# Norm statistics placed later at the heads of sublayers, and sparse-attention keys and values from 256 columns with DMA copies

## The chip, the core and the metric

The kernel runs on one core of one Trainium2 chip. The metric is the device time of one execution in microseconds, from three runs of the kernel before; the profile is of one further execution.

## The reference, cut to what matters

Two transformer blocks run one after the other on one sequence of 256 tokens and width 1024, all in float32. The first block has two layers, each with a mixer of four branches (sparse attention, retention, a linear recurrence, a short convolution), a cross-attention and an MLP. The second has an even layer (recurrence and attention, then a SwiGLU) and an odd one (gated linear attention, then eight experts). Every sublayer starts with a norm and a projection; the sparse attention takes six column groups of 64 from its projection:

```python
def rms_norm(x, g):
    xf = x.astype(jnp.float32)
    y = xf * lax.rsqrt(jnp.mean(xf * xf, axis=-1, keepdims=True) + RMS_EPS)
    return (y * g.astype(jnp.float32)).astype(x.dtype)
...
h = rms_norm(x, ln_mix_pre[l])
z = h @ w_in[l]
z_q, z_kv, z_g, z_ret, z_rwkv, z_conv, z_gate = split_cols(z, IN_SIZES)
...
k_c, v_c, k_s, v_s, k_w, v_w = jnp.split(kv, 6, axis=-1)
k_cmp = jnp.einsum('bnld,lde->bne', k_c[:, cmp_idx] + cmp_pe, cmp_w[0])
v_cmp = jnp.einsum('bnld,lde->bne', v_c[:, cmp_idx] + cmp_pe, cmp_w[1])
```

## The kernel before

**Products.** Activations lie feature-major in SBUF: a tile holds 128 features on the partitions and 256 tokens. Each float32 operand is split into a high and a low part, and a product is three matmuls: high by high, high by low, low by high. The weights stream from HBM in loads of 1 MB (`wraw`, issued by SP); each half load is one *unit*, for which ScalarE writes `whi` and VectorE `wlo` (lines 372 and 373, the *weight split*). There are four buffers of each, and `Weights.get` prepares up to three units ahead. A unit of `fm_units` gives 128 output features in 8 x 3 = 24 matmuls of 256 columns; two units fill one PSUM bank, which an eviction on VectorE then multiplies by the inverse norm. Units of `tm_units` give token-major results (`vt`, `tv`, `tg`, the cross-attention's `xv`) in two banks. PSUM has three banks for such products (tag mm) and five for the rest (tag b).

**The norm.** The gain is folded into the activations (`scaled` writes `xgh` and `xgl`), and the inverse root mean square is applied at the eviction. `squares` makes the sums of squares on ScalarE and GpSimd (`sq_acc`), `inv_rms` sums them over the partitions on TensorE (two matmuls of one column each), adds epsilon on VectorE (`st_m`) and takes the power on GpSimd (`st_tm_x`); `stat` then broadcasts the result with two matmuls and copies it to SBUF (`st_rep_x`, line 477). `later` puts all of this off to the first eviction that asks for it.

**Heads.** `ramp` takes the first three units of a sublayer and runs them side by side, chunk by chunk, since the chunks of `xgh` and `xgl` are still being made; then come their evictions, with the statistics in front. Nine sublayers begin in this way: two mixers, two cross-attentions, two MLPs, the even mixer, the SwiGLU and the odd mixer. In layer 0's mixer the ramp has one unit.

**The sparse attention.** Its projection is the units q, kcv, ksw, vt, tq, tk and so on. kcv holds the columns of k_c and v_c each twice, and ksw those of k_s and k_w each twice, so that both partition halves hold a copy: the heads lie two to a tile, on partitions 0 to 63 and 64 to 127. The additions `kp` and `vp` (line 1000) read both halves of kcv for the compression, and the scores read both halves of ksw. In layer 0, `bias_tables` also makes the position bias: a product with `c_oh`, a DMA to HBM (`bscr`), a gather back into `merged`, both issued by GpSimd (lines 775 and 777), and two products with `c_flip`.

**Order.** Engines run their instructions in order. Up to the odd layer's output product the scheduler of the tile framework may move an instruction ahead of others of its engine; `weave` sets where the steps of a branch stand between units.

Of the kernel before, what the change touches and what calls it, by code (L numbers as in the profile page):

```python
# [12 lines left out]
F32 = mybir.dt.float32  # L13
# [25 lines left out]
def _cc(w, c0, n=256):  # L39
    nb = n // P  # L40
    return w[:, c0 : c0 + n].reshape(8, P, nb, P).transpose(1, 2, 0, 3).reshape(P, 8 * n)
# [18 lines left out]
def _layout():  # L60
# [3 lines left out]
    def add(key, subs, f):  # L64
        out.append((key, subs, f))

    for l in range(2):
# [7 lines left out]
                add((nm, l, j), two, lambda a, b=base + 256 * j, wi=wi: _cc(wi(a), b))  # L75
        add(("rl", l), (1024,), lambda a, wi=wi: _cc(wi(a), 2444, 128))
        add(("q", l), two, lambda a, wi=wi: _cc(wi(a), 0))
        add(("kcv", l), two, lambda a, wi=wi: _cc(_cols(wi(a), ((256, 64), (256, 64), (320, 64), (320, 64))), 0))
        add(("ksw", l), two, lambda a, wi=wi: _cc(_cols(wi(a), ((384, 64), (384, 64), (512, 64), (512, 64))), 0))
        add(("vt", l), (560, 560), lambda a, wi=wi: _tm(_cols(wi(a), ((448, 64), (576, 64), (640, 12))), 0, 140))  # L80
        add(("tq", l), two, lambda a, wi=wi: _cc(wi(a), 652))
        add(("tk", l), two, lambda a, wi=wi: _cc(wi(a), 908))
# [304 lines left out]
class Net:  # L387
# [78 lines left out]

    def stat(self, parts, tag, copy=True):

        nc = self.nc
        tm = self.inv_rms(parts, tag)  # L470
        ps2 = self.bank()
        for h in range(2):
            self.mm(ps2[:, h * P : h * P + P], tm[:, h : h + 1].to_broadcast([P, P]), self.ident, True, True)
        if not copy:
            return ps2[:, :S], tm
        rep = (self.early if tag == "m" else self.mid).tile([P, S], F32, name="st_rep_" + tag, tag="st_rep_" + tag)
        nc.vector.tensor_copy(rep, ps2[:, :S])
        return rep, tm
# [38 lines left out]

    def later(self, sq, tag):

        made = []  # L520

        def get(i):
            if not made:
                made.extend(self.stat([sq], tag))
            return made[i]

        return (lambda: get(0)), (lambda: get(1))

    def prenorm(self):
# [68 lines left out]
    @staticmethod  # L598
    def ramp(units, n=3):

        held, out, count = [], [], 0
        for u in units:
            if u[0] != "w" or count == n:
                out.append(u)
                continue
            count += 1

            def g(hi, lo, parts=u[3].parts, last=count == n):
                held.append((parts, hi, lo))
                if not last:  # L610
                    return
                for (begin, _, _, i), _, _ in held:
                    begin(i)
                for k in range(8):
                    for (_, step, _, i), h, l in held:
                        step(i, k, h, l)
                for (_, _, end, i), _, _ in held:
                    end(i)

            out.append((*u[:3], g))  # L620
        return out

    def tm_units(self, key, xh, xl, n, evict):
# [166 lines left out]
    def mix_phase(self, l):  # L790
# [58 lines left out]
        def ev_q(ps):  # L849
# [2 lines left out]
            p3 = ps.rearrange("p (c t) -> p c t", c=2)  # L852
            nc.vector.scalar_tensor_tensor(t, p3, 0.125, rep2(), op0=ALU.mult, op1=ALU.mult)

        def ev_vt(h, ps):
            if h == 0:
                st["nv"] = st["a"].tile([P, 2, P], F32, name="nv")
# [19 lines left out]
        if l == 0:  # L877
            src.append(("x", self.load_tables))
            src.append(("x", lambda: st.__setitem__("flip", self.bias_tables(st["a"], st["merged"]))))
        src += self.fm_units(("kcv", l), xh, xl, to_fm("kcv"))  # L880
        src += self.fm_units(("ksw", l), xh, xl, to_fm("ksw"))
        src += self.tm_units(("vt", l), xh, xl, 140, ev_vt)
        units += self.ramp(src, 1 if l == 0 else 3)
        rest = []
        rest += self.fm_units(("tq", l), xh, xl, to_fm("tq"))
        rest += self.fm_units(("tk", l), xh, xl, to_fm("tk"))
        rest += self.tm_units(("tv", l), xh, xl, S, ev_tm("tv"))
        rest += self.tm_units(("tg", l), xh, xl, S, ev_tm("tg"))
# [616 lines left out]
    def xa_phase(self, l):  # L1505
# [82 lines left out]
            return f  # L1588

        qs = [self.fm_units(("xq", l, j), lambda: st["xh"], lambda: st["xl"], ev_q(j)) for j in range(4)]  # L1590
        units += self.ramp(qs[0] + qs[1])
        for j in range(4):
            if j > 1:
                units += qs[j]
# [44 lines left out]
    def mlp_phase(self, l):  # L1639
# [21 lines left out]
        done = lambda n, ps: self.post_evict(n, ps, "ln_mlp_post", l)  # L1661
        second = lambda j: self.second_product(st, ("m2", l, j), j == 0, j == 15, done, (0, 2, 4, 6, 1, 3, 5, 7))
        m1 = [self.fm_units(("m1", l, j), lambda: st["xh"], lambda: st["xl"], ev) for j in range(16)]
        units += self.ramp(m1[0] + m1[1])
        for j in range(2, 16):
            units += m1[j] + second(j - 2)
        units += second(14) + second(15)

        def close():
# [50 lines left out]
    def even_phase(self):  # L1720
# [198 lines left out]
            return [u[0] for u in us], [u[1] for u in us], fox_av(g)  # L1919

        v = [self.tm_units(("ev", j), xh, xl, S, ev_v(j)) for j in range(2)]
        units += self.ramp(fm("xr", 0) + fm("xr", 1))
        first = fm("q", 0) + fm("k", 0) + self.fm_units(("ef",), xh, xl, ev_f, nblk=1) + v[0]
        units += self.weave(first, [load, decay, conv, gates(0), gates(1)])
        a, b, c = heads(0)
        units += self.weave(fm("yr", 0) + fm("yr", 1), [lru, a[0], a[1], b[0], b[1]])
# [12 lines left out]
    def swiglu_phase(self):  # L1939
# [37 lines left out]
        for j in range(11):  # L1977
            u = self.fm_units(("f1", j), lambda: st["xh"], lambda: st["xl"], ev1)
            u += self.fm_units(("f3", j), lambda: st["xh"], lambda: st["xl"], ev3)
            units += self.ramp(u) if j == 0 else u  # L1980
            if j > 0:
                units += second(j - 1)
        units += second(10)
# [9 lines left out]
    def odd_phase(self, moe):  # L1993
# [191 lines left out]
        for j in range(4):  # L2185
            v += self.tm_units(("ov", j), xh, xl, S, ev_v(j))
            g.append(self.tm_units(("og", j), xh, xl, S, ev_g(j)))
        first = self.ramp(first)
        units += first[:5] + self.weave(first[5:], [logits, logs])
        units += self.weave(v, [decays, lambda: self.moe_load(moe), att(0), att(1)])  # L2190
        units += [("x", f) for f in (state, out(0), out(1))]
        units += g[0] + g[1] + [("x", tr(0))] + g[2] + [("x", tr(1))] + g[3] + [("x", tr(2)), ("x", tr(3))]
# [474 lines left out]
```

## Time and profile before

| | us |
|---|---|
| three runs: median (lowest, highest) | 2739.9 (2737.66, 2743.22) |
| profiled execution | 2740.58 |
| span in the profile, first to last instruction | 2738.7 |
| TensorE busy | 2656.7 |
| VectorE busy | 2073.5 |
| ScalarE busy | 1604.9 |
| GpSimd busy | 207.3 |
| mean granted TensorE clock | 0.986 |

The span is the profiled execution without what lies before its first and behind its last instruction, 1.9 us. Busy times are unions of the engine's instructions; matmuls overlap each other, so TensorE's share says that it rarely waits, not that it is at its peak. The names PE, DVE, ACT, POOL and SP in rows stand for TensorE, VectorE, ScalarE, GpSimd and the engine that issues the weight loads.

### The profile page before, as it was taken

To read this page: it belongs to the slowest core of one execution; us is meant where nothing else is said; L and a number is where in the kernel's file an instruction comes from. 1 tells how busy PE (TensorE), PEld (TensorE's weight loads), DVE (VectorE), ACT (ScalarE), POOL (GpSimd) and SP (SyncE) were. 2 spreads that over 40 slices of the span, in tenths; PEclk is the share of its full clock that TensorE was granted. 3 is DMA by queue.
4 is the path that set the end of the run, shared out by engine and by line. 5 is a ranking of instruction groups with operands and counts; after the bars stand their busy time and mean duration, and the time that the engine had idled before them with its cause. 6 is when DMAs were issued, how large, how long until landed. Compare 5 with 4: busy or idle time off the path is not lost.

```text
span 2738.7 us, 44381 instructions
## 1 busy us (share of the span) xinstructions
PE 2656.7 (97%) x17966; PEld 2420.1 (88%) x17966; DVE 2073.5 (76%) x2527; ACT 1604.9 (59%) x2140; POOL 207.3 (8%) x180
## 2 busy tenths in 40 slices
PE   8999998998999999998999999999999999999998
PEld 7989988998989998998999999887887888788876
DVE  5876765556785865556966676899999989999997
ACT  4443645444433544444654456777777777777776
POOL 1032111001022111001010010000000000000000
PEclk9999999999999999999999999999999999999999
DMA  7423434543332543454465444899999989998991
GB/s 253 146 80 132 174 140 165 184 182 136 132 110 89 180 149 123 174 184 150 142 259 211 174 168 161 339 360 350 340 351 357 359 332 358 352 361 334 366 350 68
DMA packets 99887, 614.29 MB, mean 224 GB/s; under 512 B 10521, under 2 KB 20249, under 8 KB 31705
## 3 DMA queue, kind: packets, MB, share of 16 engines
q1 hardware_dynamic: 99496, 610.83, 60.9%
q8 instruction: 143, 2.34, 0.3%
q14 instruction: 72, 0.58, 0.1%
q0 software_dynamic: 176, 0.53, 0.0%
HBM read 610.27 MB, written 1.06 MB: 223 GB/s over the span
## 4 chain that ended last, share of the span: by engine, by line
PE 48%; DVE 3%; ACT 1%; issue 1%; POOL 0%; ACTq 0%; DVEq 0%; POOLq 0%
PE ps_mm L423 31%; PE ps_b L423 16%; PE ps_b L427 1%; DVE wlo L373 1%; ACT whi L372 0%; DVE room L431 0%; DVE mt L2233 0%; DVE acc L2396 0%; POOL st_tm_x L452 0%; DVE room L2079 0%; DVE fv L2585 0%; DVE e L1841 0%; PE ps_r L2480 0%; ACT acc L2491 0%; DVE x L1714 0%
## 5 line engine op out<-in xcount | busy, mean ns | idle before, releaser
L373 DVE TENSOR_TENSOR wlo<-wraw,whi 128x1024 fp32r<-128x1024 f32 (+1 forms) x1133 | 1381.3, 1238 | 390.0 <-ACT whi L372 379.7
L372 ACT ACTIVATE whi<-wraw 128x1024 fp32r<-128x1024 f32 (+1 forms) x1133 | 1181.7, 1055 | 785.7 <-PE ps_mm L423 593.8
L423 PE MATMUL ps_mm<-xgh,whi 128*128 128x256 f32 x2080 | 601.9, 290 | 15.5 <-ACT whi L372 8.6
L423 PE MATMUL ps_mm<-xgh,wlo 128*128 128x256 f32 x2080 | 596.2, 287 | 4.1 <-DVE wlo L373 4.1
L423 PE MATMUL ps_mm<-xgl,whi 128*128 128x256 f32 x2080 | 597.4, 287 | 1.8 <-DVE xgl L507 1.8
L423 PE MATMUL ps_mm<-whi,gx 128*128 128x512 f32 x1792 | 591.1, 399 | 0.0
L423 PEld LDWEIGHTS ps_mm<-xgh,whi 128*128 128x128 f32 x2080 | 402.2, 194 | 21.5 <-ACT whi L372 8.6
L423 PEld LDWEIGHTS ps_mm<-whi,gx 128*128 128x128 f32 x1792 | 337.4, 188 | 79.4 <-issue 0.5
L423 PEld LDWEIGHTS ps_mm<-xgh,wlo 128*128 128x128 f32 x2080 | 400.1, 192 | 5.8 <-DVE wlo L373 5.5
L423 PEld LDWEIGHTS ps_mm<-xgl,whi 128*128 128x128 f32 x2080 | 400.7, 193 | 4.3 <-DVE xgl L507 3.0
L423 PE MATMUL ps_mm<-wlo,gx 128*128 128x512 f32 x896 | 354.9, 396 | 0.2 <-DVE wlo L373 0.2
L423 PE MATMUL ps_b<-whi,room 128*128 128x512 f32 x896 | 294.6, 397 | 0.0
L423 PEld LDWEIGHTS ps_mm<-wlo,gx 128*128 128x128 f32 x896 | 168.7, 188 | 39.1 <-issue 0.7
L423 PEld LDWEIGHTS ps_b<-whi,room 128*128 128x128 f32 x896 | 168.2, 188 | 39.4 <-issue 0.2
L423 PE MATMUL ps_b<-hl,whi 128*128 128x256 f32 x688 | 194.7, 283 | 0.0
L423 PE MATMUL ps_b<-hh,wlo 128*128 128x256 f32 x688 | 194.6, 283 | 0.0
L423 PE MATMUL ps_b<-hh,whi 128*128 128x256 f32 x688 | 194.6, 283 | 0.0
L423 PE MATMUL ps_b<-wlo,room 128*128 128x512 f32 x448 | 176.8, 395 | 0.0
L423 PEld LDWEIGHTS ps_b<-hh,wlo 128*128 128x128 f32 x688 | 132.0, 192 | 0.0
L423 PEld LDWEIGHTS ps_b<-hh,whi 128*128 128x128 f32 x688 | 132.0, 192 | 0.0
L423 PEld LDWEIGHTS ps_b<-hl,whi 128*128 128x128 f32 x688 | 131.9, 192 | 0.0
L423 PEld LDWEIGHTS ps_b<-wlo,room 128*128 128x128 f32 x448 | 84.2, 188 | 19.5 <-issue 0.2
(542 smaller groups left out, 3617.8 us busy)
## 6 DMA issues: line engine op xcount, KB each, us to landing
wraw<-in_w SPq DMA_DIRECT2D x559, 1024.0 KB, 5.5
wrawt<-in_w SPq DMA_DIRECT2D x32, 256.0 KB, 5.2
wraw<-in_w SPq DMA_DIRECT2D x8, 512.0 KB, 5.0
cmpw<-in_cmpw SPq DMA_DIRECT2D x2, 1024.0 KB, 4.8
mem<-in_memt SPq DMA_DIRECT2D x2, 1024.0 KB, 7.7
wraw<-in_w SPq DMA_DIRECT2D x2, 560.0 KB, 4.7
x<-in_xt SPq DMA_DIRECT2D x4, 256.0 KB, 5.0
c_rd<-in_cst SPq DMA_DIRECT2D x2, 512.0 KB, 8.2
```

The costliest lines, as they stand in the source:

```text
L372: nc.scalar.activation(hi[:, c], src[:, c], AF.Copy)
L373: nc.vector.tensor_sub(lo[:, c], src[:, c], hi[:, c].bitcast(F32))
L423: self.nc.tensor.matmul(out, lhsT, rhs, start=start, stop=stop, **kw)
L427: self.nc.tensor.transpose(out, in_, self.ident[:k, :k])
```

## The change

The sums of squares and their broadcast become two steps: `later` gives the net a function `sums`, and `spread` makes the broadcast. `opening` takes the place of `ramp` in all heads but the output products: the first three units still run side by side, the evictions of the first four units are held back, the sums stand behind the unit with number a and the held evictions, with the broadcast in front, behind the unit with number b. In MLPs, mixers and the even head a third product's units stand in between.

kcv and ksw become one product, kn, from 256 columns (k_c, v_c, k_s, k_w once each). Its eviction writes each group on the partition half where it lies, and GpSimd issues a DMA for each group that copies it to the other half. tq moves ahead of vt.

```diff
-        add(("kcv", l), two, lambda a, wi=wi: _cc(_cols(wi(a), ((256, 64), (256, 64), (320, 64), (320, 64))), 0))
-        add(("ksw", l), two, lambda a, wi=wi: _cc(_cols(wi(a), ((384, 64), (384, 64), (512, 64), (512, 64))), 0))
+        add(("kn", l), two, lambda a, wi=wi: _cc(_cols(wi(a), ((256, 64), (320, 64), (384, 64), (512, 64))), 0))
...
     def stat(self, parts, tag, copy=True):
 
+        return self.spread(self.inv_rms(parts, tag), tag, copy)
+
+    def spread(self, tm, tag, copy=True):
+
         nc = self.nc
-        tm = self.inv_rms(parts, tag)
         ps2 = self.bank()
...
-        made = []
+        tm, made = [], []
+
+        def sums():
+            if not tm:
+                tm.append(self.inv_rms([sq], tag))
 
         def get(i):
             if not made:
-                made.extend(self.stat([sq], tag))
+                sums()
+                made.extend(self.spread(tm[0], tag))
             return made[i]
 
+        self.sums = sums
...
+    def opening(self, units, n=3, a=3, held=4, b=4):
+
+
+        out, count, side, ends = [], 0, [], []
+        for u in units:
+            out.append(u)
+            if u[0] != "w":
+                continue
+            if count < held:
+                begin, step, end, i = u[3].parts
+                ends.append((end, i))
+
+                def g(hi, lo, p=u[3].parts, at=count):
+                    side.append((p, hi, lo))
+                    if at < n - 1:
+                        return
+                    for (begin, _, _, i), _, _ in side:
+                        begin(i)
+                    for k in range(8):
+                        for (_, step, _, i), h, l in side:
+                            step(i, k, h, l)
+                    side.clear()
+
+                out[-1] = (*u[:3], g)
+            if count == a:
+                out.append(("x", lambda: self.sums()))
+            if count == b:
+                out += [("x", lambda e=e: e[0](e[1])) for e in ends]
+            count += 1
         return out
...
+        def ev_kn(ps):
+
+            r = st["rep"]()
+            for i, name in enumerate(("kcv", "ksw")):
+                t = st[name] = st["a"].tile([P, 2, S], F32, name=name)
+                for j in range(2):
+                    rows, other = slice(64 * j, 64 * j + 64), slice(64 - 64 * j, 128 - 64 * j)
+                    nc.vector.tensor_mul(t[rows, j, :], ps[rows, i * S : i * S + S], r[rows, :])
+                    nc.gpsimd.dma_start(t[other, j, :], t[rows, j, :])
...
-        src += self.fm_units(("kcv", l), xh, xl, to_fm("kcv"))
-        src += self.fm_units(("ksw", l), xh, xl, to_fm("ksw"))
-        src += self.tm_units(("vt", l), xh, xl, 140, ev_vt)
-        units += self.ramp(src, 1 if l == 0 else 3)
-        rest = []
-        rest += self.fm_units(("tq", l), xh, xl, to_fm("tq"))
+        src += self.fm_units(("kn", l), xh, xl, ev_kn)
+        src += self.fm_units(("tq", l), xh, xl, to_fm("tq"))
+        units += self.opening(src, 1 if l == 0 else 3)
+        rest = self.tm_units(("vt", l), xh, xl, 140, ev_vt)
...
-        units += self.ramp(qs[0] + qs[1])
+        units += self.opening(qs[0] + qs[1], a=2, b=3)
...
-        units += self.ramp(m1[0] + m1[1])
+        units += self.opening(m1[0] + m1[1] + m1[2])
...
-        units += self.ramp(fm("xr", 0) + fm("xr", 1))
-        first = fm("q", 0) + fm("k", 0) + self.fm_units(("ef",), xh, xl, ev_f, nblk=1) + v[0]
+        units += self.opening(fm("xr", 0) + fm("xr", 1) + fm("q", 0))
+        first = fm("k", 0) + self.fm_units(("ef",), xh, xl, ev_f, nblk=1) + v[0]
...
-            units += self.ramp(u) if j == 0 else u
+            units += self.opening(u, a=2, b=3) if j == 0 else u
...
-        first = self.ramp(first)
-        units += first[:5] + self.weave(first[5:], [logits, logs])
+        first = self.opening(first, a=2, held=3, b=3)
+        units += first[:9] + self.weave(first[9:], [logits, logs])
```

What this makes of the instructions is seen in the order of the built programs. On TensorE, at the head of layer 1's mixer, the rows before are these, right behind the 72 matmuls of the first three units (a row with x2 is two instructions):

```order
L423 MATMUL ps_mm<-xgh,wlo 128x256
L423 MATMUL ps_b<-t_ident,sq_acc 128x1 x2
L423 MATMUL ps_mm<-xgh,whi 128x256
L423 MATMUL ps_mm<-xgl,whi 128x256
L423 MATMUL ps_mm<-xgh,wlo 128x256
L423 MATMUL ps_mm<-xgh,whi 128x256
L423 MATMUL ps_b<-t_ident,st_tm_x 128x128 x2
```

In the changed program the sums stand 24 matmuls further down, and 24 of tq stand between them and the broadcast, of which these are the first and the last two:

```order
L422 MATMUL ps_mm<-xgh,wlo 128x256
L422 MATMUL ps_b<-t_ident,sq_acc 128x1 x2
L422 MATMUL ps_mm<-xgh,whi 128x256
L422 MATMUL ps_mm<-xgl,whi 128x256
```

```order
L422 MATMUL ps_mm<-xgl,whi 128x256
L422 MATMUL ps_mm<-xgh,wlo 128x256
L422 MATMUL ps_b<-t_ident,st_tm_x 128x128 x2
L422 MATMUL ps_mm<-xgh,whi 128x256
```

The distance from the sums to the broadcast was four matmuls and is now a unit. On VectorE at the same head, before (wlo of 128x560 is vt's weight split):

```order
L462 TENSOR_SCALAR st_m<-ps_b 128x2
L373 TENSOR_TENSOR wlo<-wraw,whi 128x1024 x2
L477 COPY st_rep_x<-ps_b 128x256
L373 TENSOR_TENSOR wlo<-wraw,whi 128x560
L853 SCALAR_TENSOR_TENSOR nq<-ps_mm,st_rep_x 128x512
L822 TENSOR_TENSOR kcv<-ps_mm,st_rep_x 128x512
L373 TENSOR_TENSOR wlo<-wraw,whi 128x560
L860 TENSOR_SCALAR tmh<-st_tm_x 128x2
L1000 TENSOR_TENSOR kp<-kcv,prm 64x120 x4
L1000 TENSOR_TENSOR vp<-kcv,prm 64x120 x4
```

and in the changed program:

```order
L372 TENSOR_TENSOR wlo<-wraw,whi 128x1024 x2
L372 TENSOR_TENSOR wlo<-wraw,whi 128x560
L461 TENSOR_SCALAR st_m<-ps_b 128x2
L372 TENSOR_TENSOR wlo<-wraw,whi 128x560
L909 TENSOR_SCALAR tmh<-st_tm_x 128x2
L479 COPY st_rep_x<-ps_b 128x256
L372 TENSOR_TENSOR wlo<-wraw,whi 128x1024
L892 SCALAR_TENSOR_TENSOR nq<-ps_mm,st_rep_x 128x512
L901 TENSOR_TENSOR kcv<-ps_mm,st_rep_x 64x256 x2
L901 TENSOR_TENSOR ksw<-ps_mm,st_rep_x 64x256 x2
L861 TENSOR_TENSOR tq<-ps_mm,st_rep_x 128x512
L372 TENSOR_TENSOR wlo<-wraw,whi 128x1024
```

with the additions kp and vp right behind. The weight splits now stand ahead of st_m, the evictions of q, kn and tq follow each other, and kp comes three instructions behind the last of kcv's and ksw's evictions. On GpSimd, in layer 0's mixer, before:

```order
L498 TENSOR_TENSOR sq_acc<-sq_acc 128x256
L452 TENSOR_TENSOR st_tm_x<-st_m,t_ident 128x2
L775 DMA bscr<-bv 4x512
L777 DMA merged<-bscr 128x4x256
L1030 COPY scmp<-bc 128x8x17
```

and in the changed program:

```order
L500 TENSOR_TENSOR sq_acc<-sq_acc 128x256
L814 DMA bscr<-bv 4x512
L451 TENSOR_TENSOR st_tm_x<-st_m,t_ident 128x2
L816 DMA merged<-bscr 128x4x256
L902 DMA kcv<-kcv 64x256 x2
L902 DMA ksw<-ksw 64x256 x2
L1077 COPY scmp<-bc 128x8x17
```

The power now stands behind the first bias copy, and the four copies of keys and values behind the gather.

## Rows read from the trace of the kernel before

**Rows 1.** Page, part 1: busy us, share of the span, instructions of each engine.

```profile
PE 2656.7 (97%) x17966; PEld 2420.1 (88%) x17966; DVE 2073.5 (76%) x2527; ACT 1604.9 (59%) x2140; POOL 207.3 (8%) x180
```

**Rows 2.** Waits of TensorE: engine, tile, line, waited for: us, times, longest.

```profile
PE ps_b L423 <- POOL st_tm_x L452: 11.0, 8, 1.4
...
PE ps_b L423 <- POOL sq_acc L498: 6.5, 5, 1.9
```

**Rows 3.** Timeline of TensorE: start, us, instruction, in brackets the idle time before.

```profile
19.86 0.61 PE L423 MATMUL ps_b<-t_ident,sq_acc 128*128 128x1 f32 x4 [1.95 <-POOL sq_acc L498]
...
459.46 0.61 PE L423 MATMUL ps_b<-t_ident,sq_acc 128*128 128x1 f32 x4 [0.76 <-POOL sq_acc L498]
...
462.02 0.71 PE L423 MATMUL ps_b<-t_ident,st_tm_x 128*128 128x128 f32 x4 [1.38 <-POOL st_tm_x L452]
...
658.83 0.61 PE L423 MATMUL ps_b<-t_ident,sq_acc 128*128 128x1 f32 x4 [1.39 <-POOL sq_acc L498]
...
661.40 1.22 PE L423 MATMUL ps_b<-t_ident,st_tm_x 128*128 128x128 f32 x4 [1.38 <-POOL st_tm_x L452]
...
1294.21 0.61 PE L423 MATMUL ps_b<-t_ident,sq_acc 128*128 128x1 f32 x4 [1.48 <-POOL sq_acc L498]
...
1296.77 1.22 PE L423 MATMUL ps_b<-t_ident,st_tm_x 128*128 128x128 f32 x4 [1.35 <-POOL st_tm_x L452]
```

**Rows 4.** Timeline of TensorE, layer 1's mixer: kcv, first of ksw, first of vt.

```profile
663.91 0.41 PE L423 MATMUL ps_mm<-xgh,wlo 128*128 128x256 f32 x1
...
664.34 0.34 PE L423 MATMUL ps_mm<-xgl,whi 128*128 128x256 f32 x1
...
665.72 0.29 PE L423 MATMUL ps_mm<-xgh,whi 128*128 128x256 f32 x1
...
671.48 0.23 PE L423 MATMUL ps_mm<-whi,xgh 128*128 128x140 f32 x1
```

**Rows 5.** Windows at half clock: us, busy of each engine (instructions), PEclk, DMA share, GB/s.

```profile
core 0: us, PE busy (x) PEld busy (x) DVE busy (x) ACT busy (x) POOL busy (x), PEclk, DMA share, GB/s
463.07:466.48 3.41, 3.41 (x19) 3.41 (x18) 1.86 (x3) 0.03 (x1) 0.00 (x0) 0.50 0.81 283
661.04:664.46 3.42, 3.06 (x14) 3.06 (x15) 2.55 (x4) 0.00 (x0) 0.31 (x1) 0.50 0.45 113
...
1295.92:1302.75 6.83, 5.98 (x28) 5.98 (x29) 3.98 (x6) 0.67 (x1) 0.80 (x1) 0.50 0.43 156
...
sum 20.48, PE 19.27 PEld 19.27 DVE 12.97 ACT 0.69 POOL 1.10; mean PE 3.85 PEld 3.85 DVE 2.60 ACT 0.14 POOL 0.22
```

**Rows 6.** Timelines of ScalarE, GpSimd and VectorE at the MLP's and layer 1's heads.

```profile
457.90 2.96 ACT L372 ACTIVATE whi<-wraw 128x1024 fp32r<-128x1024 f32 x3 [0.66 <-PE ps_mm L423]
...
659.71 1.63 POOL L452 TENSOR_TENSOR st_tm_x<-st_m,t_ident 128x2 f32<-128x2 f32 x1 [0.94 <-DVE st_m L462]
...
665.92 0.69 DVE L822 TENSOR_TENSOR kcv<-ps_mm,st_rep_x 128x512 f32<-128x512 f32 x1 [1.59 <-PE ps_mm L423]
...
667.25 1.27 DVE L1000 TENSOR_TENSOR kp<-kcv,prm 64x120 f32<-64x120 f32 x4
```

**Rows 7.** DMA issues (KB each, us from issue to landing), and GpSimd's timeline of one.

```profile
merged<-bscr POOLq DMA_DIRECT2D x1, 512.0 KB, 9.4
...
bscr<-bv POOLq DMA_DIRECT2D x1, 8.0 KB, 2.3
...
32.16 0.81 POOL L777 DMA_DIRECT2D merged<-bscr  x1 [1.83 <-DMA bscr<-bv]
```

**Rows 8.** Timelines of VectorE and TensorE in layer 0's mixer.

```profile
17.75 3.13 DVE L373 TENSOR_TENSOR wlo<-wraw,whi 128x1024 fp32r<-128x1024 f32 x2 [2.79 <-ACT whi L372]
...
44.68 1.88 PE L423 MATMUL ps_b<-merged,c_flip 128*128 128x512 f32 x4
```

**Rows 9.** Tile xc (even mixer's convolution): ns min/median/max, first and last start.

```profile
L423 PE MATMUL ps_b<-xc,bd x16: 377/379/379, 1319.6 to 1325.6; 128*128 128x256 f32 x16
L1790 DVE SCALAR_TENSOR_TENSOR xc<-xr,prm,xc x12: 461/482/490, 1305.0 to 1317.6; 128x256 f32<-128x256 f32 x12
```

**Rows 10.** Timeline of VectorE at the even head: the decay's last step.

```profile
1294.41 0.17 DVE L1822 TENSOR_SCALAR su<-su 128x4 f32<-128x4 f32 x1
```

More of the change, by code (lines that the diff above doesn't have):

```diff
@@ L620, in ramp @@
             out.append((*u[:3], g))
+        return out
+    def opening(self, units, n=3, a=3, held=4, b=4):
[23 more added lines that the diff above has]
+            count += 1
         return out
@@ L1663, in mlp_phase @@
         m1 = [self.fm_units(("m1", l, j), lambda: st["xh"], lambda: st["xl"], ev) for j in range(16)]
-        units += self.ramp(m1[0] + m1[1])
+        units += self.opening(m1[0] + m1[1] + m1[2])
         for j in range(2, 16):
-            units += m1[j] + second(j - 2)
+            units += (m1[j] if j > 2 else []) + second(j - 2)
         units += second(14) + second(15)
```

## The prediction

> **What bounds the kernel now.** Read the busy times first: TensorE is busy 97% of the span and VectorE 76% [rows 1], so time goes away only where TensorE gets less work, waits less, or runs at a higher clock. Then read who TensorE waited for: 11.0 us in eight waits for the inverse norm st_tm_x and 6.5 us in five waits for the sum of squares sq_acc [rows 2], both in the statistics at the heads of the sublayers, 17.5 us in all. The timeline shows where they lie [rows 3]: the head of layer 0's mixer waits once, 1.95 us; the two MLP heads wait twice (0.76 and 1.38 us, the second MLP 0.87 and 1.38), as do the head of layer 1's mixer (1.39 and 1.38) and the even mixer's (1.48 and 1.35); the two cross-attentions, the SwiGLU and the odd mixer wait once, 1.38 us each (the last 1.36). Third, read the granted clock [rows 5]: right after five of these nine heads (both MLPs, layer 1's mixer, the even and the odd one) it is 0.50, for 20.48 us together, in which TensorE was busy for 19.27.
>
> **The matmuls removed.** A projection unit is 24 matmuls of 256 columns. In layer 1 the two units of ksw start at 665.72 us and the next product at 671.48: 48 matmuls in 5.76 us, 0.12 us each [rows 4]. kcv and ksw were four units and kn is two, so each layer loses 48 matmuls and the program 96: **11.5 us**. TensorE sets the end there (it waits for no weights between 664 and 672 us), so I take all of it. Nothing below zero is possible for work not done; what can come back are waits, priced below. Four weight splits and two loads of 1 MB go too, on engines that wait for TensorE.
>
> **The waits at the heads.** Each head keeps its first three units, but the column sums now stand one unit later and the broadcast of the inverse norm another unit (24 matmuls, 2.9 us) behind them. What must fit into that unit is the VectorE step st_m and GpSimd's power, 1.63 us with 0.25 before it [rows 6]; before, four matmuls stood there. The sums arrived at most 1.48 us late [rows 3], and one more unit covers that.
> - Cross-attention, twice: 1.38 us each, 2.76. The score products now stand 23 matmuls (2.8 us) behind the broadcast; the copy (0.35), a weight split (1.2), an eviction (0.65) and what they wait for add up to about 2.6. Covered, barely.
> - MLPs: 2.14 and 2.25. Here st_m is queued behind three weight splits on VectorE. In layer 0 the buffers come free at 457.90, when ScalarE's halves start [rows 6]; 1.05 us and three splits (3.4) later it is 462.4, and the inverse norm is there at 464.3. TensorE's first 72 matmuls end at 458.7 at the latest (459.46 less 0.76); two units and the sums (0.4) later, at 464.65, it comes to the broadcast. Covered by 0.4 us.
> - Layer 1's mixer: 2.77. SwiGLU 1.38, odd 1.36.
> - Even mixer: on VectorE st_m is behind three splits that start only when the decay's last small step ends, 1294.41 plus 0.17 [rows 10]; it comes at about 1298.1, the inverse norm between 0.95 (power without a split beside it, 0.7) and 1.9 us later, and TensorE is there at 1298.7. A wait of 0.4 to 1.3 us stays; I take 0.9 and count 1.9 of 2.83.
>
> Together 2.76 + 4.39 + 2.77 + 1.38 + 1.36 + 1.9 = **14.6 us**. Layer 0's mixer is counted by itself.
>
> **Layer 0's mixer.** The wait for sq_acc (1.95) was also cover. The next unit's weight split on VectorE runs from 17.75 us, two of them in 3.13 [rows 8], so TensorE can't go on before about 19.2: some 1.1 us of waiting stay. GpSimd now issues the bias copy (bscr) before the power, so the broadcast waits about 0.7 us. And the flip matmuls, at 44.68 before [rows 8], come up at about 38.4, since 48 matmuls fewer stand ahead of them. They need the bias gather, issued at 32.16 and landed 9.4 us later [rows 7]; its issue moves only to about 30, so it lands at about 39.3: 0.9 us of waiting. 1.1 + 0.7 + 0.9 - 1.95 = 0.75 us **lost**.
>
> **The clock.** In a half-clock stretch a 256-column matmul takes 0.215 us (663.91 to 664.34 is two), at full clock 0.12 [rows 4]; a microsecond of busy half clock is worth 1 - 0.12/0.215 = 0.44 us. What TensorE did before each of these falls was wait twice, or once in the odd head; the longer waits of the sublayer's end lie before an earlier fall, which I leave alone. Where all of the head's waits go, I expect the fall to go: 1.5 us for each MLP, 1.35 for layer 1's mixer (3.06 us busy), 1.5 for the odd head, 5.9 us. After the even head (5.98 us busy) it is 2.6, but then TensorE comes to the gate products, at 1319.6 before [rows 9], 4.5 us earlier, and VectorE's convolution, whose last step starts at 1317.6, ends only about 1.5 us earlier: 1.4 us of that goes into a wait. I count 1.2, so **7.1 us**. The Trainium skill, "TensorE: Matmul & The Clock Gate" (Terms), prices a throttled stretch at its length times one half, which would be 10.2 us for the 20.48 where the rows say 8.5 (19.27 times 0.44); the stretches hold some idle time, and the measured spacing decides.
>
> **The copies of keys and values.** kn's eviction is four VectorE operations on 64 partitions instead of two on 128 (0.69 each [rows 6]); priced between half and the whole of that row, 1.4 to 2.8 us against 1.4; the splits behind them have a unit or more (2.9 us) in hand: nothing. Then GpSimd issues four copies, 0.8 us each [rows 7], ahead of nothing that is due soon. The eight kp and vp additions wait for the two kcv copies, and behind them on VectorE are the weight splits. Counted as if layer 1's head began at its old time: the first 72 matmuls end at 657.4 (658.83 less 1.39 [rows 3]), the broadcast at 664.0; then the copy, a split, nq and two evictions on VectorE, to 667.1, and GpSimd issues the second copy by 668.5. The nearest rows for its landing are 2.3 us (bscr, 8 KB) and 9.4 (the gather, 512 KB); a copy has 64 KB, little traffic is under way, and I take 3. Then the additions (2.55 us) end at 674 and the next split at 675.3, while TensorE works through vt and tk until 677.9: hidden, and hidden up to a landing of 5.6 us. In layer 0 the copies queue behind the gather and land at about 40; additions end at 42.7, where the compression stands at 47. Cost nothing.
>
> **Sum.** 11.5 + 14.6 + 7.1 - 0.75 = 32.4 us. The profiled execution took 2740.6 us (span 2738.7, 1.9 around it), 0.7 above the median of 2739.9, so from 2740.6: **2708 us**. What comes after 1730 us, the experts, is untouched.
>
> **Rivals.**
> 1. *The clock does not come back*: the falls only move, or come from the waits of the sublayer's end, which stay. For it: four heads waited 1.4 to 1.95 us without a fall. Against it: all five falls begin in or within 1.1 us of a head's last wait (463.07 and 661.04 against 462.02 and 661.40 [rows 3, 5]). Without the 7.1 us: 2715.
> 2. *The copies land late and hold VectorE.* At 9.4 us [rows 7] in both layers, 3.8 us beyond the cover each: 7.6 us, 2716. For it: the gather waited that long. Against it: bscr landed in 2.3 while VectorE was at the same additions. The Trainium skill, "SBUF — State Buffer" (two separate sides), says that GpSimd cannot write descriptors while VectorE runs a copy in a two-port mode; it speaks for this rival. The list of operations in that page (Who interferes with whom) says that a tensor_tensor has no such mode, and bscr's row agrees with it: the Trainium skill would thus leave this rival small.
> 3. *The waits move instead of going*: evictions held back to one burst leave PSUM full, or st_m stays behind splits at every head. Then only the matmuls count, with the 0.75: 2730.
> 4. *Slower.* The copies again, by one mechanism: VectorE stands at the kp additions and TensorE runs out of split weights. Beyond 5.6 us every microsecond of landing costs one in each layer, so 32.4 us are eaten, and 5.5 more lost (2746), at 5.6 + 37.9/2 = 25 us. The slowest GpSimd copy in the trace took 9.4.
>
> **Numbers.** Forecast 0.62 (2702 to 2712); rival 1 0.16; rival 2 0.10; rival 3 0.07; rival 4 0.02; 0.03 for a gain that some other wait eats to within 0.2%, about what a measurement of this kernel can tell from no change. The range starts at 2700, where the falls at the sublayers' ends get shorter too by one stretch each (four times 1.5 us), and ends at 2722, which takes in rivals 1 and 2 and nearly both at once; rival 3 and the rest are left out. Faster by over 0.2%: 0.95; within 0.2%: 0.03; slower: 0.02.
>
> **What would show it.** Right: 96 fewer matmuls of 256 columns; TensorE's waits for st_tm_x and sq_acc fall from 17.5 us to under 5; no half-clock stretch behind the MLP, layer 1 and odd heads; kp's additions wait for kcv's copy, and no whi or wlo wait of TensorE follows. Wrong: waits of TensorE for wlo behind kp, for a PSUM bank at the heads, for merged at the flip over 2 us, or 0.50 in the clock at the same five places.

## The result, and the profile after

The changed kernel took 2709.1 us (median of four runs, 2706.8 to 2712.8) against 2739.3 of the kernel before in the same sitting: ratio 0.9889, 95% interval 0.9872 to 0.9906. In a second sitting it was 2710.8, ratio 0.9891 (0.9875 to 0.9908). The forecast of 2708 holds, but two of its terms were off: the clock's by about half, and layer 0's mixer in its sign.

The page's first part, as [rows 1], and then TensorE's waits, as [rows 2]:

```profile
PE 2643.1 (98%) x17870; PEld 2405.5 (89%) x17870; DVE 2068.0 (76%) x2527; ACT 1601.1 (59%) x2136; POOL 213.5 (8%) x188
```

```profile
PE ps_mm L422 <- DVE wlo L372: 7.3, 10, 1.1
...
PE ps_b L422 <- POOL st_tm_x L451: 1.1, 2, 0.9
...
PE ps_mm L422 <- DVE gt L1012: 0.8, 1, 0.8
PE ps_b L422 <- DVE fc L1826: 0.8, 1, 0.8
```

TensorE has the 96 matmuls less. Its waits for the sums are gone, those for the inverse norm fell from 11.0 to 1.1 us; new are one more wait for wlo (ten, 7.3 us, for nine, 6.3), one for gt (a gate in layer 1's mixer) and one for fc (the even mixer's decay). At the linear recurrences of both layers TensorE waited 3.3 us for the power inv before; here it waits 3.1 for ScalarE's sq. Span less busy time gives TensorE's idle time, 82.0 us before and 64.7 now, 17.3 less; its busy time fell by 13.6, 2.1 more than 96 matmuls are worth at full clock.

TensorE's timeline at the heads, to compare with [rows 3] (layer 0's mixer up to 37.56, layer 1's at 647 to 651, the even mixer's behind 1270):

```profile
18.31 0.39 PE L422 MATMUL ps_mm<-xgh,wlo 128*128 128x256 f32 x1 [0.99 <-DVE wlo L372]
...
25.80 0.61 PE L422 MATMUL ps_b<-t_ident,sq_acc 128*128 128x1 f32 x4
28.60 0.71 PE L422 MATMUL ps_b<-t_ident,st_tm_x 128*128 128x128 f32 x4
37.56 1.98 PE L422 MATMUL ps_b<-merged,c_flip 128*128 128x512 f32 x4
...
647.56 0.50 PE L422 MATMUL ps_b<-t_ident,sq_acc 128*128 128x1 f32 x4
...
650.88 0.61 PE L422 MATMUL ps_b<-t_ident,st_tm_x 128*128 128x128 f32 x4
...
1274.47 0.71 PE L422 MATMUL ps_b<-t_ident,st_tm_x 128*128 128x128 f32 x4 [0.94 <-POOL st_tm_x L451]
```

A row without brackets waited for nothing. Of the nine heads only the even one still waits for the inverse norm to speak of, 0.94 us; the first MLP's waits 0.15.

The clock: two stretches at heads, which stood at 0.50 in [rows 5] (the second row is layer 1's mixer), and then three of the eight half-clock stretches that are left, with the sum over all eight (columns as in [rows 5]):

```profile
447.00:457.00 10.00, 9.85 (x82) 9.64 (x82) 6.90 (x7) 5.65 (x6) 4.55 (x4) 1.00 0.40 147
645.00:655.00 10.00, 10.00 (x87) 10.00 (x86) 7.33 (x12) 4.07 (x6) 1.52 (x3) 1.00 0.59 210
```

```profile
765.60:775.84 10.24, 10.24 (x50) 8.56 (x48) 6.72 (x16) 5.48 (x15) 2.85 (x3) 0.50 0.33 112
...
1308.32:1318.56 10.24, 10.24 (x46) 8.89 (x45) 8.34 (x14) 6.23 (x19) 0.00 (x0) 0.50 0.29 102
1339.04:1342.45 3.41, 3.41 (x18) 3.41 (x18) 3.31 (x4) 0.47 (x1) 0.00 (x0) 0.50 0.45 190
sum 58.00, PE 48.91 PEld 43.84 DVE 49.23 ACT 29.15 POOL 16.35; mean PE 6.11 PEld 5.48 DVE 6.15 ACT 3.64 POOL 2.04
```

All five stretches behind the heads are gone, 20.48 us. But the sum over all stretches fell only from 64.84 to 58.00 us: the stretch in layer 1's linear recurrence (765 us) grew from 3.41 to 10.24, and two in the even mixer (1308 and 1339) are new. (Left out of both sums is a stretch at the end of the program in which no matmul runs, 9.2 us before and 6.9 now.) Of the kernel before, the stretch in the recurrence and the sum:

```profile
790.75:794.16 3.41, 3.01 (x15) 2.71 (x13) 3.41 (x12) 3.23 (x10) 1.67 (x2) 0.50 0.74 291
...
sum 64.84, PE 52.13 PEld 49.16 DVE 48.41 ACT 21.75 POOL 17.03; mean PE 4.34 PEld 4.10 DVE 4.03 ACT 1.81 POOL 1.42
```

Before the stretch at 1308, TensorE and VectorE of the changed kernel show this:

```profile
1301.62 1.13 PE L422 MATMUL ps_b<-k,q 64*128 64x256 f32 x8
1305.56 1.99 PE L422 MATMUL ps_b<-fc,c_sel 8*128 8x256 f32 x8 [0.82 <-DVE fc L1826]
```

```profile
1304.84 0.67 DVE L1826 TENSOR_TENSOR_SCAN fc<-t_ident,fz 8x256 f32<-8x256 f32 x1
```

The 0.82 us are new; at the same place the kernel before waited for nothing:

```profile
1332.76 1.99 PE L423 MATMUL ps_b<-fc,c_sel 8*128 8x256 f32 x8
```

VectorE, without a pause since 1275 us, ends the decay fc when its own queue lets it, and TensorE is now there first.

The copies: issues as in [rows 7], and VectorE at the additions kp in layer 0 and layer 1.

```profile
merged<-bscr POOLq DMA_DIRECT2D x1, 512.0 KB, 5.8
kcv<-kcv POOLq DMA_DIRECT2D x4, 64.0 KB, 3.4
```

```profile
37.72 0.62 DVE L1047 TENSOR_TENSOR kp<-kcv,prm 64x120 f32<-64x120 f32 x2 [1.89 <-DMA kcv<-kcv]
...
657.34 1.29 DVE L1047 TENSOR_TENSOR kp<-kcv,prm 64x120 f32<-64x120 f32 x4
```

VectorE waited once, 1.89 us in layer 0, and TensorE did not notice.

### The profile page after: what moved, and what is told of

Same layout as the page of the kernel before. It is cut to its first block, busy times and chain, and to the rows that moved or that the text cites. A ratio compares the mean times of both kernels' runs of the same rounds, so it can differ in the third digit from the quotient of the medians.

```text
span 2707.8 us, 44209 instructions
## 1 busy us (share of the span) xinstructions
PE 2643.1 (98%) x17870; PEld 2405.5 (89%) x17870; DVE 2068.0 (76%) x2527; ACT 1601.1 (59%) x2136; POOL 213.5 (8%) x188
## 3 DMA queue, kind: packets, MB, share of 16 engines
q0 software_dynamic: 432, 1.06, 0.1%
HBM read 608.17 MB, written 1.06 MB: 225 GB/s over the span
## 4 chain that ended last, share of the span: by engine, by line
PE 49%; DVE 2%; ACT 1%; issue 0%; POOL 0%; ACTq 0%
PE ps_mm L422 32%; PE ps_b L422 16%; PE ps_b L426 1%; DVE wlo L372 1%; ACT whi L371 0%; DVE room L430 0%; DVE mt L2280 0%; DVE acc L2443 0%; DVE room L2126 0%; DVE fv L2632 0%; ACT acc L2538 0%; DVE x L1761 0%; ACT room L2106 0%; PE ps_r L2527 0%; DVE xgl L509 0%
## 5 line engine op out<-in xcount | busy, mean ns | idle before, releaser
L422 PE MATMUL ps_mm<-xgh,whi 128*128 128x256 f32 x2048 | 591.1, 289 | 14.5 <-ACT whi L371 7.7
L422 PE MATMUL ps_mm<-xgh,wlo 128*128 128x256 f32 x2048 | 585.0, 286 | 5.1 <-DVE wlo L372 5.1
L422 PE MATMUL ps_mm<-xgl,whi 128*128 128x256 f32 x2048 | 586.0, 286 | 1.8 <-DVE xgl L509 1.8
L422 PEld LDWEIGHTS ps_mm<-xgh,whi 128*128 128x128 f32 x2048 | 393.7, 193 | 20.4 <-ACT xgh L508 8.0
L422 PEld LDWEIGHTS ps_mm<-xgh,wlo 128*128 128x128 f32 x2048 | 391.7, 191 | 7.0 <-DVE wlo L372 6.7
L422 PEld LDWEIGHTS ps_mm<-xgl,whi 128*128 128x128 f32 x2048 | 392.0, 191 | 4.6 <-DVE xgl L509 3.0
```

What stands on the lines that cost most here:

```text
L422: self.nc.tensor.matmul(out, lhsT, rhs, start=start, stop=stop, **kw)
```

## The experiments

All medians stand beside the kernel before in the same sitting (2740.6, then 2740.0, then 2742.0). Since runs of one kernel differ in granted clock, a second reading is used: a run's half-clock time is twice (1 - clock) times its time, each microsecond of it costs 0.44 by the prediction's rows, so the time at full clock is the time less 0.88 x (1 - clock) of it. It is an estimate: the clock is given to three digits (1.2 us of rounding in a run), and TensorE is not busy in all of the half-clock time (52.1 of 74.0 us in the profile before, 48.9 of 64.9 in the changed one's first, end of the program included). So the last column is too high in every row, and differences of one or two microseconds in the last two columns say little. The means:

| | runs | mean us | granted clock | at full clock | cost of the clock |
|---|---|---|---|---|---|
| before | 33 | 2739.9 | 0.9866 | 2707.6 | 32.3 |
| changed | 8 | 2709.8 | 0.9880 | 2681.2 | 28.6 |
| kn alone | 16 | 2732.3 | 0.9851 | 2696.4 | 35.9 |
| later statistics alone | 5 | 2720.5 | 0.9874 | 2690.3 | 30.2 |
| copies late | 5 | 2719.1 | 0.9860 | 2685.6 | 33.5 |
| sums early | 4 | 2714.0 | 0.9878 | 2684.7 | 29.3 |
| even head back | 4 | 2708.2 | 0.9888 | 2681.4 | 26.8 |
| scores later | 8 | 2705.0 | 0.9894 | 2679.7 | 25.3 |

**kn alone.** The kernel before, with kn's weights and its eviction `ev_kn` as in the changed kernel and

```diff
-        src += self.fm_units(("kcv", l), xh, xl, to_fm("kcv"))
-        src += self.fm_units(("ksw", l), xh, xl, to_fm("ksw"))
+        src += self.fm_units(("kn", l), xh, xl, ev_kn)
```

> One part alone: the kernel before, with its heads as they were, and only the product kn with its four copies in the place of kcv and ksw (vt stays behind it). By the prediction's terms the 96 matmuls are the whole of it: 2739.3 less 11.5, so 2728, with TensorE's eight waits for the inverse norm and five for the sums as in [rows 3], and no wait for whi or wlo behind the additions kp. If the copies hold VectorE (rival 2), up to 7.6 us of it are lost: 2731 to 2735. If something besides the matmuls was gained through kn, below 2726.

Measured 2733.2, ratio 0.9975 (0.9964 to 0.9987): 7 us instead of 11.5. Its seven times lay far apart, so it was run again:

> The same kernel as the run with kn alone, whose seven times fell into two groups (2726.4 and 2726.6; 2732.8 to 2736.5), for a second profile. If the groups are two patterns of the granted clock, the profiles' half-clock stretches differ by some 15 us between them at the same waits. If they are late copies, a profile of the slower group shows VectorE waiting for kcv's copy ahead of kp, and TensorE for wlo behind it.

Measured 2732.7, 0.9976 (0.9965 to 0.9987), nine times from 2728.3 to 2737.1: no two groups, a spread. The profiles of the two sittings are of one and the same program; their executions took 2726.4 and 2731.0 us, and their half-clock stretches add up to 61.4 and 75.1, 13.7 more in the second. At the heads of the second cross-attention, the SwiGLU and the odd mixer both wait 1.37 or 1.38 us for the inverse norm, as here at the cross-attention, first profile and second:

```profile
986.49 0.71 PE L422 MATMUL ps_b<-t_ident,st_tm_x 128*128 128x128 f32 x4 [1.38 <-POOL st_tm_x L451]
```

```profile
988.98 0.87 PE L422 MATMUL ps_b<-t_ident,st_tm_x 128*128 128x128 f32 x4 [1.38 <-POOL st_tm_x L451]
```

The windows behind the three waits, in the first profile and in the second:

```profile
986.00:996.00 10.00, 9.51 (x73) 9.30 (x74) 7.02 (x9) 3.06 (x6) 0.44 (x1) 1.00 0.59 210
1394.00:1404.00 10.00, 9.83 (x82) 9.83 (x83) 8.06 (x10) 4.28 (x6) 1.42 (x2) 1.00 0.75 266
1587.00:1597.00 10.00, 9.70 (x81) 9.70 (x82) 6.51 (x9) 3.20 (x4) 0.24 (x1) 1.00 0.62 215
```

```profile
989.39:992.80 3.41, 3.41 (x18) 3.41 (x17) 2.26 (x4) 0.00 (x0) 0.00 (x0) 0.50 0.63 214
...
1395.58:1398.99 3.41, 3.41 (x18) 3.41 (x17) 2.16 (x3) 0.00 (x0) 0.00 (x0) 0.50 0.76 238
1590.14:1593.55 3.41, 3.41 (x19) 3.41 (x18) 2.48 (x4) 0.00 (x0) 0.00 (x0) 0.50 0.80 300
```

The same waits are followed by full clock in one execution and by half clock in the other; no wait of TensorE for wlo behind kp stands in either. At full clock kn alone gains 11.2 us, the prediction's 11.5; it gives 3.6 back because its clock is lower on average. One of the added falls has its place: behind the wait of 1.95 us at layer 0's head, where the profile before stays at full clock, all three profiles with the old heads and kn (the next run's too) have 3.41 us at 0.50, from 19.7 or 20.0 us. Why this program falls more often than the one before is not shown.

**kn alone, tq first.** As above, with tq moved ahead of vt:

```diff
+        src += self.fm_units(("tq", l), xh, xl, to_fm("tq"))
         units += self.ramp(src, 1 if l == 0 else 3)
+        rest = self.tm_units(("vt", l), xh, xl, 140, ev_vt)
```

> The kernel before with its heads as they were, kn with its four copies, and tq ahead of vt as in the changed kernel (the run with kn alone had vt behind kn). If the 96 matmuls are worth their 11.5 us and the run with kn alone lost some 4 of them because the two units behind kn were vt's: 2728 to 2729. If kn gives only about 7 wherever the heads are those of before: 2733 again, and what is missing comes back only together with the later statistics.

Measured 2729.5, 0.9966 (0.9954 to 0.9978), six times from 2722.5 to 2734.5; 2696.4 at full clock, as without the move. The difference between the two is in the clock (0.9863 against 0.9851), and the intervals overlap: what the move of tq does by itself stays undecided.

**Later statistics alone.** The changed kernel with kcv and ksw as before:

```diff
-        src += self.fm_units(("kn", l), xh, xl, ev_kn)
-        src += self.fm_units(("tq", l), xh, xl, to_fm("tq"))
+        src += self.fm_units(("kcv", l), xh, xl, to_fm("kcv"))
+        src += self.fm_units(("ksw", l), xh, xl, to_fm("ksw"))
```

> The other part alone: the heads of the changed kernel (sums and broadcast later), but kcv and ksw as two products of 512 columns without copies, as before. By the prediction's terms: 14.6 us of waits and 7.1 of clock, and in layer 0 no early flip, so about 2739.3 - 21.7 = 2717.6. If the clock gives back only the 3 us that the two profiles' half-clock stretches differ by, 2721 to 2722. The two parts alone and the changed kernel should then add up: the gains of this run and of the run with kn alone together 30 us; more or less than 30 by over 3 says that the parts help or hinder each other.

Measured 2720.8, 0.9927 (0.9913 to 0.9941), close to the second of the two expectations. The parts' medians give 7.4 + 19.8 = 27.1 of the changed kernel's 30.1, on the bound of 3; at full clock they give 11.2 + 17.3 = 28.5 where the changed kernel has 26.4, the other way round. So the parts add up to within 3 us, and whether they help or hinder each other is not decided. The waits in front of the two linear recurrences do not decide it either: 0.8 us here and 3.1 in the changed kernel's first profile, but 1.9 in its second, and 1.7 and 0.2 in the two of kn alone.

**Copies late.** Each copy by three transfers in a row:

```diff
-                    nc.gpsimd.dma_start(t[other, j, :], t[rows, j, :])
+                    nc.gpsimd.dma_start(scr[0, 2 * i + j], t[rows, j, :])
+                for j in range(2):
+                    nc.gpsimd.dma_start(scr[1, 2 * i + j], scr[0, 2 * i + j])
+                for j in range(2):
+                    nc.gpsimd.dma_start(t[64 - 64 * j : 128 - 64 * j, j, :], scr[1, 2 * i + j])
```

> The changed kernel, with each copy of keys and values going by three transfers in a row (to HBM, within HBM, back to the other partition half), so that kcv's copies land roughly 12 us behind their eviction instead of about 4, and ksw's behind them. By the prediction's cover of 5.6 us of landing in layer 1 that is some 6 us late there, and about as much in layer 0: 2709 + 6 to 12 = 2715 to 2721, with waits of TensorE for wlo behind kp. If the cover is far larger than 5.6 us (the additions are early and the order on VectorE leaves slack): within 2 us of 2709.

Measured 2717.6, 0.9926 (0.9912 to 0.9939): 8.4 us more by the medians (9.3 by the means), as expected, but not where expected. VectorE's timeline, layer 0 and layer 1, then TensorE's:

```profile
46.95 0.36 DVE L1052 TENSOR_TENSOR kp<-kcv,prm 64x120 f32<-64x120 f32 x1 [10.43 <-DMA kcv<-kns]
...
673.81 0.65 DVE L1052 TENSOR_TENSOR kp<-kcv,prm 64x120 f32<-64x120 f32 x2 [4.42 <-DMA kcv<-kns]
```

```profile
47.36 1.10 PE L422 MATMUL ps_b<-kp,cmpw 128*64 128x15 f32 x16 [1.78 <-DVE kp L1052]
...
56.09 0.39 PE L422 MATMUL ps_b<-kc,t_rot 64*128 64x15 f32 x2 [1.95 <-DVE kc L1064]
...
675.16 2.04 PE L422 MATMUL ps_b<-kp,cmpw 128*64 128x15 f32 x32
```

In layer 1 the copies landed 9.8 us behind their first issue (664.01), some 9.2 behind the second, from which the prediction counts. VectorE waited 4.42 us and TensorE didn't: the cover there is 9.2 us at least, not 5.6. It is not much more, since TensorE came to the compression (675.16) 0.7 us behind the last of the kp additions. In layer 0 they landed 14.4 us behind theirs (32.58); TensorE waited 4.3 us for kp and kc, and right behind, the clock went to 0.50 for 3.41 and 6.83 us (from 49.99 and 56.82). By this profile the loss is layer 0's: 4.3 us of waits where the table has 4.4 at full clock, and 10.2 us of half clock, some 4.5, where it has 4.9 of clock. It came through the compression's own matmuls, not through splits queued on VectorE; the expected waits for wlo behind kp did not come.

**Sums early.** The changed kernel with the sums back behind the third unit in the MLPs, layer 1's mixer and the even mixer:

```diff
-    def opening(self, units, n=3, a=3, held=4, b=4):
+    def opening(self, units, n=3, a=2, held=4, b=4):
...
-        units += self.opening(src, 1 if l == 0 else 3)
+        units += self.opening(src, 1 if l == 0 else 3, a=3 if l == 0 else 2)
```

> The changed kernel, with the sums of squares back behind the third unit at the four heads that waited twice (both MLPs, layer 1's mixer, the even mixer); the broadcast stays where the change put it, two units later. The waits for sq_acc should come back as in [rows 3], 0.76, 0.87, 1.39 and 1.48, 4.5 us, and none for st_tm_x. Theory of the prediction (the clock falls with the head's waits, and a fall needs more than what one wait makes): half-clock stretches stay away from these heads, 2709 + 4.5 = 2713.6. Rival (one wait at the head is enough for a fall): stretches of 3.4 us behind the heads come back, 1.5 us each, 2717 to 2719. If the wait at the even head for st_tm_x (0.94) goes away as well, 0.9 less in both.

Measured 2713.9, 0.9904 (0.9889 to 0.9919). TensorE at the first MLP's head, and the windows there, at layer 1's head and at the even head:

```profile
452.77 0.61 PE L422 MATMUL ps_b<-t_ident,sq_acc 128*128 128x1 f32 x4 [1.09 <-POOL sq_acc L500]
...
459.08 0.61 PE L422 MATMUL ps_b<-t_ident,st_tm_x 128*128 128x128 f32 x4
```

```profile
451.00:461.00 10.00, 8.90 (x75) 8.70 (x74) 5.97 (x7) 4.95 (x5) 3.27 (x3) 1.00 0.39 140
648.00:658.00 10.00, 9.39 (x79) 9.18 (x78) 5.23 (x8) 4.30 (x5) 3.12 (x3) 1.00 0.42 156
1271.00:1281.00 10.00, 8.63 (x73) 8.43 (x72) 8.00 (x12) 4.52 (x5) 3.11 (x3) 1.00 0.41 147
```

Waits for the sums came back (1.09, 0.61, 0.55 and 1.36 us, 3.6 for the expected 4.5), those for the inverse norm did not, and no head fell to 0.50: the prediction's side, in one profile. With the runs of kn alone beside it this is a tendency and no rule, since there one wait of 1.38 was enough in three places of one execution.

**Even head back.** The changed kernel with the even head as before:

```diff
-        units += self.opening(fm("xr", 0) + fm("xr", 1) + fm("q", 0))
-        first = fm("k", 0) + self.fm_units(("ef",), xh, xl, ev_f, nblk=1) + v[0]
+        units += self.ramp(fm("xr", 0) + fm("xr", 1))
+        first = fm("q", 0) + fm("k", 0) + self.fm_units(("ef",), xh, xl, ev_f, nblk=1) + v[0]
```

> The changed kernel with the even mixer's head as before (three units, then sums, broadcast and evictions), all else as changed. By the prediction that head was worth 1.9 us of waits and 1.2 of clock: 2709 + 3.1 = 2712. Theory from the profiles: what the even head gains is taken back some 30 us further on, where TensorE comes to the first attention scores before VectorE has the decay (fc) and then runs 10 us at half clock; with the head back, that wait and that stretch go away again and the half clock behind the head returns: 2709 within 1.5.

Measured 2708.2, 0.9885 (0.9869 to 0.9900): no different from the changed kernel. The head's waits and its half clock are back (first two rows and window), the wait for fc and the stretch at 1308 are gone:

```profile
1268.35 0.61 PE L422 MATMUL ps_b<-t_ident,sq_acc 128*128 128x1 f32 x4 [1.49 <-POOL sq_acc L500]
1270.92 1.22 PE L422 MATMUL ps_b<-t_ident,st_tm_x 128*128 128x128 f32 x4 [1.38 <-POOL st_tm_x L451]
...
1306.91 1.99 PE L422 MATMUL ps_b<-fc,c_sel 8*128 8x256 f32 x8
```

```profile
1270.00:1276.83 6.83, 5.91 (x27) 5.91 (x28) 3.98 (x6) 0.60 (x1) 0.87 (x1) 0.50 0.42 154
```

TensorE comes to the fc matmuls at 1306.9 here and at 1305.6 in the changed kernel: what the even head gains is handed to VectorE's chain. All five profiles that have the opened even head and the scores in their old place (two of the changed kernel, later statistics alone, copies late, sums early) have the wait for fc, 0.82 or 0.83 us, and a stretch of 6.8 to 13.7 us at half clock right behind it; this run has neither.

**Scores later.** The changed kernel with q's second product ahead of the first scores' softmax:

```diff
-        units += self.weave(fm("yr", 0) + fm("yr", 1), [lru, a[0], a[1], b[0], b[1]])
-        units += self.weave(fm("q", 1) + fm("k", 1), [c, gelu])
+        units += self.weave(fm("yr", 0) + fm("yr", 1) + fm("q", 1), [lru, a[0], a[1], b[0], b[1]])
+        units += self.weave(fm("k", 1), [c, gelu])
```

> The changed kernel with the two units of q's second product moved ahead, so that the first attention scores of the even mixer stand one unit (2.9 us) later and their softmax up to two units later. Theory: the wait for fc (0.82) goes and the scores lie apart, so that the clock does not fall to 0.50 at 1308 us (10.24 us there, worth 4.5): 2704 to 2706. Rival: VectorE's chain (busy without a break from 1275 to 1317 us) sets the pace of this stretch whatever TensorE's clock is, and the time comes back as waits or a fall elsewhere in the even mixer: 2709 within 1.5.

Measured 2705.2, 0.9877 (0.9862 to 0.9892). It was run once more beside the changed kernel, on one chip:

> The changed kernel once more, for times beside the next run on the same chip and for a second profile. Expected 2709 as before, ratio 0.988 to 0.990; no half-clock stretch at the nine heads; the stretch behind the first attention scores of the even mixer (10.24 us at 1308 in the first profile) there again, with the wait for fc of 0.8; the stretches of the linear recurrence and of the sublayers' ends at the same places with other lengths.

> The run with the first attention scores one unit later once more, beside the changed kernel on the same chip. If the 4 us between them (2705.2 against 2709.1, taken in two sittings) are real: 3 to 5 us below the changed kernel here too. If they were a difference between sittings: within 1.5.

Measured 2710.8 for the changed kernel and 2704.8 with the scores later, ratio 0.9867 (0.9851 to 0.9884): 5.9 us in this sitting, and 4.8 by the means of eight runs each. The gain is real, and this is the fastest version here. In the changed kernel's second profile the wait for fc (0.82) was there again and the stretch behind the scores was 6.83 us, at 1307.48. With the scores later, in the second profile:

```profile
1305.08 1.13 PE L422 MATMUL ps_b<-k,q 64*128 64x256 f32 x8
1306.15 1.99 PE L422 MATMUL ps_b<-fc,c_sel 8*128 8x256 f32 x8
...
1320.47 1.06 PE L426 MATMUL ps_b<-t_ident,fs 128*128 128x128 f32 x8 [0.98 <-DVE fs L744]
```

```profile
1303.00:1313.00 10.00, 10.00 (x76) 8.60 (x75) 10.00 (x17) 6.47 (x7) 0.00 (x0) 1.00 0.30 105
```

There the fc matmuls wait for nothing and the clock stays at 1.00; at the softmax TensorE waits 0.98 us. In the first profile of this kernel they wait for nothing either, but the clock still fell to 0.50 for 3.41 us, from 1308.96. So the wait went in both profiles, and the stretch became shorter or went; that the wait alone makes the stretch is not shown. VectorE did not set the pace alone, as the rival had it: product work put ahead of the scores gained time.

## Why the prediction was right, by its steps

- **The matmuls removed (11.5).** Right: 96 fewer [rows 1], and 11.2 us at full clock with kn alone.
- **The waits at the heads (14.6).** Right. The even head waits 0.94 us where 0.9 was kept, and seven heads do not wait for it. The bare cover at the cross-attentions held. At the first MLP the 0.4 us in hand became a wait of 0.15: its three splits on VectorE, counted as 3.4 us, took 4.24 (from 448.73), and the power ended at 454.73, when TensorE had been there since 454.64.
- **Layer 0's mixer (0.75 lost).** Wrong in sign; it gained about 1 us. The wait for wlo came (0.99 for the estimated 1.1). The 0.7 at the broadcast did not: the power started at 27.65, right behind the bias copy's issue, and TensorE reached the broadcast only at 28.60. Nor did the 0.9 at the flip, and that was luck: the gather was issued at 31.68 and not at about 30, TensorE came to the flip at 37.56 and not at 38.4 (which is also half a microsecond earlier than the 48 matmuls, 5.8 us, give), and only a landing in 5.8 us instead of the 9.4 of [rows 7] left nothing to wait for; with 9.4 it would have been 3.5 us.
- **The clock (7.1).** Its first half was right: where the head's waits went, the falls went, in every profile with the later statistics. The size failed: 3.7 us came back on average. The step that failed is "I count 1.2" for the even head. The 1.4 us of waiting that it expected at the gate products showed up as 0.82 at fc, further on; the price left out was the half clock right behind it, 10.24 us in one profile and 6.83 in the other, some 4.5 and 3.0 us, and in the first profile 3.41 more at 1339. The five falls at the heads were worth 8.5; less 6.0 and 3.0 that leaves 2.5 and 5.5, around the 3.7 measured. With the even head back the time is the same, so this head was worth nothing. The stretches elsewhere, "which I leave alone", do not keep their length from one execution to the next: outside the heads, layer 0's mixer, the even mixer's scores and the end of the program they add up to 41.0 to 54.6 us in the eight profiles with the later statistics and to 41.0 to 47.8 in the four without, so the growth of one of them in the first profile (765 us) is no effect that these runs show.
- **The copies (nothing).** Right, with 1.89 us of VectorE waiting in layer 0. The evictions took 0.41 to 0.43 each, 1.7 together, in the range given, and GpSimd issued a copy in 0.53 us for the 0.8 counted. The cover was mis-sized: 9.2 us or more in layer 1 for 5.6.
- **The sum.** At full clock 26.4 us for 25.4 (11.5 + 14.6 - 0.75), and 3.7 for 7.1 of clock: 30.1 for 32.4. So the total is nearer than its terms: layer 0's mixer, 1.7 us better than forecast, made up for some half of what the clock lacked. The range's lower end has a slip: four stretches of 1.5 us below 2708 are 2702, not 2700.
- **The rivals.** The first, that the clock does not come back, was half true: "the falls only move" is what happened to the even head's, which came back at the next place where TensorE met VectorE, while the other four heads' falls went. The second and fourth were tested by the late copies: even landings of 9.2 us cost layer 1 nothing, so the fourth's price of one microsecond for each beyond 5.6 was too high there. Layer 0, with landings of 14.4 us, did pay, by waits at the compression and not at the weight splits. The Trainium skill, "DMA: Bandwidth & Descriptors" (Anatomy of one DMA), gives a transfer issued by GpSimd about 2.0 us plus its bytes over 436 GB/s, 2.15 us by that estimate for 64 KB; the medians here went from 2.0 us (ksw, kn alone) to 3.4 (kcv, changed kernel), single copies from 1.9 to 5.2, so it fits the shortest and says nothing of the rest. The third did not happen.

## What to carry to other kernels

When a wait at a head is hidden, ask where the engine arrives earlier and who is due there: the next meeting with a busy VectorE took back all that the even head gave, and one product put ahead of that place gained some 5 us more. In these runs a wait of about a microsecond was followed, in some executions, by 3.4 to 13.7 us of half clock, so compare kernels by time and by granted clock, over many runs, before a few microseconds are put down to an edit. How late a copy may land was set by the place of its consumer on TensorE, and it took a kernel with late copies to measure it.

## What the runs showed of the hardware

The granted clock after a wait of 1.38 us was 1.00 in one execution and 0.50 for 3.41 us in another of the same program, at three heads; runs of this one program went from 2726.4 us (clock 0.987) to 2737.1 (0.983). The 512 KB gather landed 9.4 us behind its issue in the profile before and 4.0 to 7.5 in the other eleven, the 64 KB copies 2.0 to 3.4 in the median. GpSimd took 1.06 us to issue two copies, 0.53 each, where its issue of the gather took 0.81 [rows 7].
